# The causal masks of a state space scan: from a second TensorE product to a ScalarE copy in a PSUM bank of their own

## The chip, the cores and the metric

One core of a Trainium2 chip runs the whole program. The metric is the device time of one execution in microseconds (us). A matmul is issued on TensorE (PE, with its weight loads PEld); VectorE is DVE, ScalarE is ACT, GpSimd is POOL, SyncE is SP, and SP alone issues the transfers (DMA).

## The reference, cut to what matters

Two blocks follow each other. The first (attention with an index, latent attention, memory attention, experts in groups) ends before the change begins. The second has two layers: a bidirectional state space mixer (SSD) with an expert-choice layer (16 experts of 1024x1024, f32), then attention with a second expert-choice layer. The change lies in the SSD, of which this is the core:

```python
acum = jnp.cumsum(a, axis=-1)
tri = jnp.tril(jnp.ones((Q, Q), dtype=bool))
seg = jnp.exp(jnp.where(tri, acum[..., :, None] - acum[..., None, :], -jnp.inf))
cb = jnp.einsum('bclgn,bcsgn->bcgls', Cc, Bc)
y_diag = jnp.einsum('bcgrls,bcsgrp->bclgrp', cb[:, :, :, None] * seg, xdt)
```

It runs for context and latent tokens (256 each, chunks of 128), forwards and backwards, in 8 groups of 4 heads. `seg` on a diagonal chunk needs the causal mask, triangular one way for the forward scan and the other way for the backward scan.

## The kernel before, in words

The program is recorded in Python, and a scheduler then sets the order of each engine's instructions by its own simulated times: an instruction is placed when it would be ready, in favour of what was written earlier. So an edit at one place moves instructions of all engines from there on. Everything ahead of the SSD stands as before.

PSUM has eight banks of 128 x 512 f32. `self.ps(tag)` takes the next bank of a tag, `self.pb` says how many each tag has. From the SSD to the end of the first expert-choice layer the division is p=2, y=2, b=2, t=2 (`run`).

The SSD loops over the groups g = 0 to 7. `ssd_project` (L1462 on) makes six pieces of 128 channels: each splits its weights into a high and a low part (`split`, L1294 on ACT and L1295 on DVE, tiles `ws`, two buffers), multiplies them with the tokens in 24 matmuls (`mm3`, L1300 to L1302, tag p), and runs a five-tap convolution (ACT `pad`, `conv`, `xbc`; DVE L1506). `ssd_group` (L1522 on) transposes the pieces (tag t: L1530, L1535), makes `cb` (L1550, tag b) and then loops over the latent or context half q and the two chunks st. For each of these four steps it makes three exponents: two on the diagonal (d = 0 forwards, d = 1 backwards) and one off it. One exponent is a matmul into a bank of tag b (L1561, tiles `LBg` and `RR`); on the diagonal a second matmul adds the mask (L1564, `identb` times `maskb`, both bf16); ACT then takes the exponential into an SBUF tile `seg` (L1566, three buffers). POOL adds the two diagonal ones (L1568), DVE multiplies by `cb` into `M` (L1571), and TensorE applies M to the inputs (L1574, tag y). State products (L1586, L1592, L1597), sums and the spill of the group's result follow. While TensorE does group g's steps it also does the projections of group g+1, in the order that the scheduler set.

After the last group come the output projection (`ssd_out`, weights split again by L1294 and L1295, matmuls L1300 to L1302), the routing of the experts (tags t and b) and the expert products (L1817, tags p and y), whose weights arrive in `w` slots.

Of the kernel before, what the change touches and what calls it, by code (L numbers as in the profile page):

```python
# [22 lines left out]
AF = mybir.ActivationFunctionType  # L23
# [55 lines left out]
class Net:  # L79
# [11 lines left out]

    def ps(self, tag, n=512, dt=F32):
        self.n += 1
        return self.pp.tile([P, n], dt, tag=tag, name=f"ps{self.n}", bufs=self.pb[tag])

    @contextmanager
# [1214 lines left out]
    def ssd(self, right):  # L1311
        nc, a = self.nc, self.a
        self.piece = -1
        with self.pool("ssdh") as hp, self.pool("ssdx") as xp, self.pool("ssd") as pool, ExitStack() as q:
            tile_, x_ = self.cut(pool), self.cut(xp)
            pp = q.enter_context(self.pool("ssdq", "right"))
            self.ada_tile, self.ada_ps = lambda: self._t(pp, [P, 2 * D], "adaw", 1), "p"
            hT = [self.cut(hp)([P, 8, 512], f"hT{v}", 1, F32R) for v in range(2)]
            for r, xx in ((1, self.ctx_x), (0, self.x)):
                rows = self.norm_halves([xx[:, 0], xx[:, 1]], lambda: x_([P, 512], "xbc", 8), self.ctx_r if r else None)  # L1320
                m, sh = self.mod_cols(0, 0, r)
                self.to_features_mod(rows, m, sh, hT, (1 - r) * T, lambda: x_([P, 512], "z", 4)[:, :T])
            with self.pool("ssdr") as rp:
                self.load_const("const_b", rp)
                tmp_ = self.cut(rp)
                A4 = self.arena(rp, 3)
                self.ada_step(1)
                self.ssd_steps(tile_, tmp_, A4, hT)
            with self.pool("ssdg") as gp:
                self.yd = [self.dp.tile([P, 2, 512], F32, name=f"yd{g}") for g in range(7)]  # L1330
                self.sqa = self.cut(gp)([P, 512], "sqa")
                nc.gpsimd.memset(self.sqa, 0.0)
                for g in range(8):
                    parts = self.ssd_project(g, self.cut(pp), self.cut(xp), hT)
                    if g == 7:
                        q.close()
                        op = right.enter_context(self.pool("ssdo", "right"))
                        self.y7 = self.cut(op)([P, 2, 512], "y7")
                    self.ssd_group(g, *parts, self.cut(gp), self.cut(op) if g == 7 else None)
        return self.cut(op), op  # L1340
# [182 lines left out]
    def ssd_group(self, g, xs, BT, CT, zz, tile_, last=None):  # L1523
        nc = self.nc
# [21 lines left out]
        for q in range(2):  # L1546
# [7 lines left out]
            for st in range(2):  # L1554
# [2 lines left out]

                for d, var, lt, diag in ((0, 2 * q + st, st, True), (1, 2 * q + st, st, True),
                                         (st, 4 + q, 1 - st, False)):
                    p = self.ps("b").rearrange("p (r l) -> p r l", r=4)  # L1560
                    nc.tensor.matmul(p, lhsT=LBg[d][:, var * P:(var + 1) * P], rhs=self.RR[d][:, :, 2 * q + lt],  # L1561
                                     start=True, stop=not diag)
                    if diag:
                        nc.tensor.matmul(p, lhsT=self.identb, rhs=self.maskb[:, d], start=False, stop=True)  # L1564
                    e = tile_([P, 4, P], "seg", 3)
                    nc.scalar.activation(e, p, AF.Exp)  # L1566
                    ex.append((e, lt))
# [503 lines left out]
    def run(self):  # L2071
# [2 lines left out]
        self.small = "b"  # L2074
        nc = self.nc
        four = dict(p=2, y=2, b=2, t=2)
        with ExitStack() as right, self.psum(**four):
            out_, _ = self.ssd(right)
            ap = self.ctx.enter_context(self.pool("attt"))
            with self.pool("ch0") as pool, self.weight_slots(2), ExitStack() as more:  # L2080
# [71 lines left out]
```

## Time and profile before

| | us |
|---|---|
| median of 3 runs | 2182.82 |
| lowest, highest | 2179.14, 2183.91 |
| the profiled execution | 2178.93 |
| its span | 2177.1 |

The profile is of one execution. A page gives busy time by engine and 40 slices; a table by stage gives busy time, granted TensorE clock (PEclk, 1.00 is 2.4 GHz) and the share of DMA time for stretches that one chooses; a list of waits names the instruction that ended an engine's idle time. An instruction's duration on TensorE is not its cost in a full stream, since matmuls overlap: there the distance of the starts counts.

### The profile page before, as it was taken

How to read it: one execution, taken by the hardware profiler on the slowest of the kernel's cores; microseconds unless marked ns; L12 is line 12 of the kernel's file. 1: busy time of each engine (PE TensorE's matmuls, PEld its weight loads, DVE VectorE, ACT ScalarE, POOL GpSimd, SP SyncE). 2: the span in 40 equal slices, each digit the busy share in tenths (PEclk: the TensorE clock that was granted, in tenths of full speed). 3: DMA queues.
4: the chain of work that ended last, by engine and by line, in shares of the span. 5: the costliest groups of instructions: out<-in, count | busy, mean ns of one | idle time of the engine just before them, and what ended most of it. 6: DMA issues, size and time to landing. Idle time of an engine off the chain costs nothing. (4 is left out here: it accounts for less than half of the span.)

```text
span 2177.1 us, 23487 instructions
## 1 busy us (share of the span) xinstructions
PE 1882.8 (86%) x9000; PEld 1026.5 (47%) x9000; DVE 964.0 (44%) x1627; ACT 633.5 (29%) x1174; POOL 459.6 (21%) x481
## 2 busy tenths in 40 slices
PE   7989879988999999799899999997989767767666
PEld 6767644356767776567433333333756311111111
DVE  6776532278777777666222222222666301010101
ACT  6554421264444555444000000002454200000000
POOL 4340110033323333521011111111743100000000
PEclk9999989999999999999899999998999889898999
DMA  7554839843322222275799999997538699999996
GB/s 235 194 200 151 313 139 385 339 142 104 114 88 84 91 90 68 91 262 202 315 427 427 427 428 426 427 427 300 205 127 306 285 428 427 427 428 428 428 425 278
DMA packets 128565, 603.48 MB, mean 277 GB/s; under 512 B 18123, under 2 KB 58734, under 8 KB 87998
## 3 DMA queue, kind: packets, MB, share of 16 engines
q1 hardware_dynamic: 128446, 601.91, 69.8%
q8 instruction: 73, 1.20, 0.2%
q14 instruction: 46, 0.38, 0.1%
HBM read 597.09 MB, written 4.78 MB: 276 GB/s over the span
## 5 line engine op out<-in xcount | busy, mean ns | idle before, releaser
L1817 PE MATMUL ps<-w,xg 128*64 128x512 f32 (+1 forms) x2048 | 458.9, 648 | 106.1 <-DMA w<-in_moe_w_dram 106.1
L1817 PEld LDWEIGHTS ps<-w,xg 128*64 128x64 f32 (+1 forms) x2048 | 133.2, 129 | 392.8 <-issue 238.8
L1870 POOL TENSOR_TENSOR x<-x,o 128x512 f32<-128x512 f32 x24 | 38.9, 1623 | 651.2 <-DVE o L1869 651.2
L1300 PE MATMUL ps<-hT,ws 128*128 128x512 f32 x384 | 156.9, 409 | 6.3 <-DVE ada L1235 6.1
L1301 PE MATMUL ps<-hT,ws 128*128 128x512 f32 x384 | 156.9, 409 | 0.0
L1302 PE MATMUL ps<-hT,ws 128*128 128x512 f32 x384 | 155.3, 404 | 0.0
L1817 PE MATMUL ps<-w,ctx 128*32 128x512 f32 x512 | 109.1, 645 | 37.6 <-DMA w<-in_moe_w_dram 36.7
L1860 DVE SCALAR_TENSOR_TENSOR y<-ps,s,y 128x512 fp32r<-128x512 f32 x24 | 17.9, 748 | 247.5 <-ACT y L1859 247.5
L1817 PE MATMUL ps<-w,actT 128*64 128x512 f32 x512 | 123.5, 595 | 1.9 <-ACT actT L1855 1.9
L1506 DVE SCALAR_TENSOR_TENSOR conv<-pad,cols,conv 128x512 f32<-128x512 f32 x124 | 111.9, 903 | 2.6 <-ACT conv L1499 0.4
L1859 ACT ACTIVATE y<-ps,s 128x512 fp32r<-128x512 f32 x24 | 16.5, 686 | 322.8 <-PE ps L1817 246.4
L1300 PEld LDWEIGHTS ps<-hT,ws 128*128 128x128 f32 x384 | 72.7, 189 | 27.5 <-DVE ada L1235 6.8
L1869 DVE TENSOR_TENSOR o<-ps,g 128x512 f32<-128x512 f32 x80 | 52.3, 686 | 69.3 <-PE ps L1866 65.8
L1295 DVE TENSOR_TENSOR ws<-wr,ws 128x1024 fp32r<-128x1024 f32 x48 | 62.3, 1299 | 44.6 <-ACT ws L1294 38.0
L1301 PEld LDWEIGHTS ps<-hT,ws 128*128 128x128 f32 x384 | 72.8, 190 | 19.0 <-issue 3.8
L1302 PEld LDWEIGHTS ps<-hT,ws 128*128 128x128 f32 x384 | 72.7, 189 | 18.0 <-issue 1.9
L1817 PEld LDWEIGHTS ps<-w,ctx 128*32 128x32 f32 x512 | 25.9, 114 | 115.5 <-DMA w<-in_moe_w_dram 60.6
L1817 PEld LDWEIGHTS ps<-w,actT 128*64 128x64 f32 x512 | 43.4, 136 | 71.5 <-issue 67.0
L1568 POOL TENSOR_TENSOR seg<-seg,seg 128x512 f32<-128x512 f32 x32 | 47.4, 1481 | 116.1 <-ACT seg L1566 101.3
L1295 DVE TENSOR_TENSOR ws<-w,ws 128x1024 fp32r<-128x1024 f32 x46 | 61.5, 1343 | 19.9 <-ACT ws L1294 19.5
L1566 ACT ACTIVATE seg<-ps 128x512 f32<-128x512 f32 x96 | 54.8, 597 | 51.0 <-PE ps L1564 26.9
L1571 DVE TENSOR_TENSOR M<-seg,cb 128x512 f32<-128x512 f32 x64 | 53.7, 854 | 31.0 <-ACT seg L1566 20.7
(639 smaller groups left out, 3644.9 us busy)
## 6 DMA issues: line engine op xcount, KB each, us to landing
w<-in_moe_w_dram SPq DMA_DIRECT2D x164, 2048.0 KB
w<-in_moe_w_dram SPq DMA_DIRECT2D x56, 1024.0 KB
v<-in_ada_w_dram SPq DMA_DIRECT2D x16, 1024.0 KB
w<-in_moe_w_up_dram SPq DMA_DIRECT2D x16, 1024.0 KB
w<-in_moe_w_gate_dram SPq DMA_DIRECT2D x16, 1024.0 KB
w<-in_moe_w_down_dram SPq DMA_DIRECT2D x16, 1024.0 KB
wr<-in_ssd_in_w_dram SPq DMA_DIRECT2D x16, 1024.0 KB
w<-in_ssd_out_w_dram SPq DMA_DIRECT2D x32, 512.0 KB
```

The lines of the kernel that those rows point to most:

```text
L1295: (eng or self.nc.vector).tensor_tensor(lo, x, hi.bitcast(F32), op=OP.subtract)
L1300: t.matmul(p, lhsT=L[0], rhs=R[0], start=start, stop=False, **kw)
L1301: t.matmul(p, lhsT=L[0], rhs=R[1], start=False, stop=False, **kw)
L1302: t.matmul(p, lhsT=L[1], rhs=R[0], start=False, stop=stop, **kw)
L1506: nc.vector.scalar_tensor_tensor(seq(cv), pad[:, :, j:j + 256], tap(j), seq(cv), op0=OP.mult, op1=OP.add)
L1566: nc.scalar.activation(e, p, AF.Exp)
L1568: nc.gpsimd.tensor_tensor(ex[0][0], ex[0][0], ex[1][0], op=OP.add)
L1571: nc.vector.tensor_tensor(M[:, :, s], e, cb[:, st, None, s].to_broadcast([P, 4, P]), op=OP.mult)
L1817: nc.tensor.matmul(p[j * S:(j + 1) * S], lhsT=x(k, j), rhs=ws[j // ne][:, j % ne, k % nk, n * 512:(n + 1) * 512], start=(k == 0), stop=(k ...
L1860: nc.vector.scalar_tensor_tensor(y[:, 1], p, ws, y[:, 0].bitcast(F32), op0=OP.mult, op1=OP.subtract)
L1869: nc.vector.tensor_tensor(o, q, gr[s][:, c], op=OP.mult)
L1870: (nc.gpsimd if i else nc.vector).tensor_tensor(xx[:, i, c], xx[:, i, c], o, op=OP.add)
```

## The change

The masks of the diagonal exponents are no longer added by a matmul. One PSUM bank (tag m, tile `self.seg`) is set aside for all diagonal exponents. The very first time the mask goes in by the old identity matmul; the other 63 times ACT copies it from `maskb` into the bank (L1567 of the new file), and the exponents' matmul (L1568) adds onto it instead of starting afresh. Off-diagonal exponents stay on tag b. The division of the banks becomes p=2, y=2, b=3, m=1, from the SSD to the end of the first expert-choice layer; a tag that a division lacks, t here, falls to b.

```diff
     def ps(self, tag, n=512, dt=F32):
         self.n += 1
+        tag = tag if tag in self.pb else "b"
...
                 self.ssd_steps(tile_, tmp_, A4, hT)
+
+            self.seg = self.ps("m").rearrange("p (r l) -> p r l", r=4)
...
-                    p = self.ps("b").rearrange("p (r l) -> p r l", r=4)
+                    p = self.seg if diag else self.ps("b").rearrange("p (r l) -> p r l", r=4)
+                    if diag and (g, q, st, d) == (0, 0, 0, 0):
+                        nc.tensor.matmul(p, lhsT=self.identb, rhs=self.maskb[:, d], start=True, stop=True)
+                    elif diag:
+                        nc.scalar.activation(p, self.maskb[:, d], AF.Copy)
                     nc.tensor.matmul(p, lhsT=LBg[d][:, var * P:(var + 1) * P], rhs=self.RR[d][:, :, 2 * q + lt],
-                                     start=True, stop=not diag)
-                    if diag:
-                        nc.tensor.matmul(p, lhsT=self.identb, rhs=self.maskb[:, d], start=False, stop=True)
+                                     start=not diag, stop=True, skip_group_check=True)
...
-        with ExitStack() as right, self.psum(**four):
+        with ExitStack() as right, self.psum(p=2, y=2, b=3, m=1):
```

How the order moves: in the new file L1301 to L1303 are the projections (L1300 to L1302 before), L1533 the transposes (L1530), L1553 `cb` (L1550), L1568 the exponents (L1561), L1571 the exponentials (L1566), L1579 the products with M (L1574); the bank set aside is `ps1379_6544`.

On TensorE, the start of the fourth group, before (1790 is a projection, 1786 the modulation product that shares its banks):

```order
L1233 MATMUL ps1786_8460<-adaw_1785_8458,silu_c_336 32x512 x2
L1530 MATMUL ps1704_8109<-const_75,xbc_1672_7902 128x128 x4
L1561 MATMUL ps1717_8142<-RR0_1351_6452,LBg_1708_8126 128x512
L1564 LDWEIGHTS identb_1331_6366
L1564 MATMUL ps1717_8142<-maskb_1332_6368,identb_1331_6366 128x512
L1561 MATMUL ps1719_8147<-RR1_1369_6510,LBg_1710_8130 128x512
L1564 LDWEIGHTS identb_1331_6366
L1564 MATMUL ps1719_8147<-maskb_1332_6368,identb_1331_6366 128x512
L1530 MATMUL ps1705_8115<-const_75,xbc_1678_7944 128x128 x4
L1233 MATMUL ps1786_8460<-adaw_1785_8458,silu_c_336 32x512 x2
L1300 MATMUL ps1790_8472<-hT0_1281_6199,ws0_1788_8468 128x512
```

The two diagonal exponents of a step stand side by side in two banks, each with its mask, and a projection follows.

TensorE in the fourth group now, between the end of one projection (1763) and the start of the next (1816):

```order
L1303 MATMUL ps1763_8473<-hT0_1281_6199,ws1_1762_8470 128x512
L1553 MATMUL ps1691_8113<-xbc_1668_8008,xbc_1662_7966 128x256 x2
L1568 MATMUL ps1379_6544<-RR1_1369_6510,LBg_1687_8107 128x512
L1568 MATMUL ps1696_8127<-RR0_1351_6452,LBg_1685_8103 128x512
L1568 MATMUL ps1701_8147<-RR1_1369_6510,LBg_1687_8107 128x512
L1553 MATMUL ps1703_8158<-xbc_1668_8008,xbc_1662_7966 128x256 x2
L1568 MATMUL ps1708_8172<-RR0_1351_6452,LBg_1685_8103 128x512
L1568 MATMUL ps1379_6544<-RR0_1351_6452,LBg_1685_8103 128x512
L1579 MATMUL ps1689_8111<-M_1693_8118,xtm_1680_8085 64x256 x2
L1579 MATMUL ps1690_8112<-M_1693_8118,xtm_1680_8085 64x256 x2
L1568 MATMUL ps1379_6544<-RR1_1369_6510,LBg_1687_8107 128x512
L1301 MATMUL ps1816_8676<-hT0_1281_6199,ws0_1814_8672 128x512
```

Three diagonal exponents stand here with no projection between them, all in the one bank.

On ACT, the same place before:

```order
L1566 ACTIVATE seg_1718_8145<-ps1717_8142 128x512
L1566 ACTIVATE seg_1720_8150<-ps1719_8147 128x512
L1612 ACTIVATE xbc_1579_7478<-xbc_1579_7478,cols1_314 128x512
L1531 ACTIVATE xtm_1703_8108<-ps1705_8115 128x512
L1612 ACTIVATE xbc_1585_7520<-xbc_1585_7520,cols1_314 128x512
```

and now:

```order
L1295 ACTIVATE ws0_1820_8714<-wr_1818_8710 128x1024
L1556 ACTIVATE cb_1692_8116<-ps1691_8113 128x512
L1571 ACTIVATE seg_1695_8125<-ps1379_6544 128x512
L1571 ACTIVATE seg_1697_8129<-ps1696_8127 128x512
L1567 ACTIVATE ps1379_6544<-maskb_1332_6368 128x512
L1556 ACTIVATE cb_1704_8161<-ps1703_8158 128x512
L1511 ACTIVATE xbc_1747_8382<-conv_1746_8376 128x512
L1611 ACTIVATE z_1590_7634<-xbc_1564_7463 128x512
L1571 ACTIVATE seg_1699_8141<-ps1379_6544 128x512
L1611 ACTIVATE z_1594_7666<-xbc_1570_7505 128x512
L1617 ACTIVATE xbc_1564_7463<-xbc_1564_7463,cols1_314 128x512
L1567 ACTIVATE ps1379_6544<-maskb_1332_6368 128x512
```

Each copy stands behind the exponential that empties the bank, with other work of ACT between.

On TensorE, the start of the last group, before:

```order
L1561 MATMUL ps2091_9852<-RR0_1351_6452,LBg_2082_9836 128x512
L1564 LDWEIGHTS identb_1331_6366
L1564 MATMUL ps2091_9852<-maskb_1332_6368,identb_1331_6366 128x512
L1530 MATMUL ps2079_9825<-const_75,xbc_2050_9640 128x128 x4
L1561 MATMUL ps2093_9857<-RR1_1369_6510,LBg_2084_9840 128x512
```

and now:

```order
L1568 MATMUL ps1379_6544<-RR1_1369_6510,LBg_1942_9355 128x512
L1533 MATMUL ps2024_9770<-const_75,xbc_1995_9585 128x128 x4
L1538 MATMUL ps2026_9777<-const_75,xbc_2002_9630 128x128 x2
L1568 MATMUL ps1379_6544<-RR0_1351_6452,LBg_2027_9781 128x512
L1553 MATMUL ps2033_9791<-xbc_2008_9672,xbc_2002_9630 128x256 x2
L1579 MATMUL ps1944_9359<-M_1965_9431,xtm_1935_9333 64x256 x2
L1579 MATMUL ps1945_9360<-M_1965_9431,xtm_1935_9333 64x256 x2
L1568 MATMUL ps1379_6544<-RR1_1369_6510,LBg_2029_9785 128x512
```

The last group has no projection left beside it, before or now; its eight diagonal exponents now pass through the one bank.

## Rows read from the trace of the kernel before

**Rows 1.** The page, busy time by engine over the span.

```profile
PE 1882.8 (86%) x9000; PEld 1026.5 (47%) x9000; DVE 964.0 (44%) x1627; ACT 633.5 (29%) x1174; POOL 459.6 (21%) x481
```

**Rows 2.** By stage: length, busy of PE, PEld, DVE, ACT, POOL; clock, DMA, GB/s.

```profile
510.00:860.00 350.00, 346.44 (x1611) 252.29 (x1611) 269.14 (x330) 176.21 (x289) 107.86 (x140) 1.00 0.28 85
...
860.00:913.00 53.00, 43.43 (x198) 26.54 (x197) 34.13 (x41) 25.41 (x45) 27.69 (x28) 0.94 0.34 111
913.00:1024.00 111.00, 104.09 (x466) 81.82 (x465) 74.10 (x106) 52.17 (x71) 25.24 (x20) 1.00 0.59 202
1024.00:1042.00 18.00, 8.29 (x37) 5.07 (x37) 10.28 (x31) 5.56 (x8) 5.38 (x3) 0.70 0.98 398
...
1056.00:1400.00 344.00, 321.45 (x1326) 121.75 (x1323) 82.53 (x169) 26.90 (x49) 38.24 (x29) 0.98 1.01 426
```

**Rows 3.** TensorE by line, 510 to 860: count, busy and mean ns, idle before.

```profile
L1301 PE MATMUL ps<-hT,ws 128*128 128x512 f32 x330 | 135.3, 410 | 0.0
...
L1561 PE MATMUL ps<-RR,LBg 128*128 128x512 f32 x76 | 33.0, 460 | 0.0
...
L1564 PE MATMUL ps<-maskb,identb 128*128 128x512 bf16 x51 | 19.9, 390 | 0.0
```

**Rows 4.** TensorE in order of time near 859: start, duration, instruction.

```profile
858.41 0.39 PE L1300 MATMUL ps<-hT,ws 128*128 128x512 f32 x1
858.64 0.40 PE L1561 MATMUL ps<-RR,LBg 128*128 128x512 f32 x1
858.88 0.39 PE L1564 MATMUL ps<-maskb,identb 128*128 128x512 bf16 x1
858.92 0.58 PE L1301 MATMUL ps<-hT,ws 128*128 128x512 f32 x1
...
859.34 0.39 PE L1302 MATMUL ps<-hT,ws 128*128 128x512 f32 x1
```

**Rows 5.** Waits of TensorE, 510 to 860: total, times, longest.

```profile
PE ps L1300 <- DVE ada L1235: 3.2, 1, 3.2
```

**Rows 6.** ACT by line, 510 to 860: count, busy and mean ns, idle before.

```profile
L1294 ACT ACTIVATE ws<-wr 128x1024 fp32r<-128x1024 f32 x41 | 43.3, 1057 | 49.5 <-PE ps L1301 49.2
L1566 ACT ACTIVATE seg<-ps 128x512 f32<-128x512 f32 x75 | 42.8, 598 | 38.3 <-PE ps L1564 22.1 <-PE ps L1561 14.8 <-POOL seg L1568 1.0
L1499 ACT ACTIVATE conv<-ps,cols,cols 128x512 f32<-128x512 f32 x28 | 21.7, 774 | 2.2 <-DVE xbc L1509 2.2
L1508 ACT ACTIVATE xbc<-conv 128x512 f32<-128x512 f32 x27 | 17.1, 633 | 42.6 <-DVE conv L1506 29.1 <-issue 10.0 <-DMA yd<-xbc 3.4
L1496 ACT ACTIVATE pad<-ps 128x512 f32<-128x512 f32 x28 | 16.3, 582 | 0.4 <-ACT eF L1594 0.4
```

**Rows 7.** By stage, columns as in rows 2: behind the wait, and in the tail.

```profile
645.00:650.00 5.00, 5.00 (x15) 3.98 (x16) 4.76 (x7) 1.47 (x4) 0.02 (x1) 0.66 0.54 150
650.00:655.00 5.00, 5.00 (x26) 3.28 (x26) 2.21 (x3) 3.06 (x5) 1.39 (x3) 1.00 0.25 61
...
895.00:902.00 7.00, 5.98 (x20) 2.96 (x22) 2.36 (x3) 2.39 (x4) 1.61 (x2) 0.53 0.00 0
```

**Rows 8.** The last two groups in order of time, with idle time before.

```profile
866.36 1.02 PE L1550 MATMUL ps<-xbc,xbc 128*128 128x256 f32 x4
...
895.37 0.69 DVE L1571 TENSOR_TENSOR M<-seg,cb 128x512 f32<-128x512 f32 x1 [1.73 <-POOL seg L1568]
...
902.67 0.39 PE L1564 MATMUL ps<-maskb,identb 128*128 128x512 bf16 x1
...
903.10 1.08 ACT L1566 ACTIVATE seg<-ps 128x512 f32<-128x512 f32 x2 [1.22 <-PE ps L1564]
903.75 0.50 PE L1561 MATMUL ps<-RR,LBg 128*128 128x512 f32 x1 [0.46 <-ACT seg L1566]
903.84 1.28 POOL L1568 TENSOR_TENSOR seg<-seg,seg 128x512 f32<-128x512 f32 x1 [6.52 <-ACT seg L1566]
...
912.74 0.59 PE L1300 MATMUL ps<-ws,y 128*128 128x512 f32 x1
```

## The prediction

> **What bounds the kernel now.** First the page: TensorE is busy for 86% of the span, more than any other engine [rows 1], but that is an average. So the next view is the table by stage [rows 2]. In 510 to 860 us, the stretch in which groups one to seven are worked off, TensorE is busy for 346.4 of 350 us at the full clock, DVE for 269, ACT for 176, POOL for 108, and the transfers take 28%: TensorE sets the pace. In 860 to 913, the last two groups, nothing is full; there a chain from engine to engine sets the end. In 913 to 1024 the output projection keeps TensorE busy for 104 of 111 us. From 1024 to 1042 the latent tokens are routed, a chain on DVE and ACT, and from 1056 the weights of the experts stream at 1.01 of the transfer engines' time. That stream begins only when the slots are free and the routed tokens are there, and then runs at a fixed rate; so a microsecond won or lost before it comes out at its end. The waits of TensorE in 510 to 860 are one of 3.2 us [rows 5] and some tenths: there is no slack in which a removed product could vanish.
>
> **What the products of the mask cost.** Of the 64, 51 lie in 510 to 860 [rows 3]. Their duration of 390 ns is not their price, since matmuls overlap. From the start of the L1561 at 858.64 to that of the L1302 at 859.34 three matmuls pass, the mask's among them, in 0.70 us: 0.233 us each, as much as a projection's [rows 4], and no more for the change of type. 51 x 0.233 = 11.9 us, all of it on the path while TensorE is full. One product stays, before 510. The other 12 lie in the last two groups, where TensorE waits anyway: I count nothing for them, 12 x 0.233 = 2.8 us at the best.
>
> **What the copies cost.** ACT gains 63 copies of 128x512. The trace has no ACT write to PSUM; the nearest rows are a copy from PSUM (582 ns), the exponentials (598), a function from SBUF to SBUF (633) and one with two column operands (774) [rows 6]. I take 0.60, nearest to the plain ones, with 0.58 and 0.77 as the ends. In 510 to 860 that is 51 x 0.6 = 31 us, and ACT goes from 176 to 207 of some 340 us. It does not become the bound; the time is hidden under TensorE's projections, as long as ACT gets to a copy before TensorE gets to the product that waits for it.
>
> **The new wait.** One bank now holds every diagonal exponent in turn: copy, product, exponential, and only then the next copy. The shortest turn is 0.60 + 0.43 (from the start of a product to the exponential behind it, 902.67 to 903.10) + 0.58 and two handovers of under 0.1 us [rows 8]: about 1.75 us, 14 us for a group's eight turns, against some 48 us that a group has. What counts is therefore where the order puts the next product. TensorE executes in order, so behind a waiting L1568 all projections are queued, and ACT's weight splits and DVE wait for these. In the new order most diagonal products before the last two groups stand 20 to 35 rows apart, 4.6 to 7.7 us at 0.233 a matmul. ACT's work between, typically a split (1.06), a copy for the convolution (0.58), its scaled copy (0.77), an exponential and the mask's copy (0.6 each), takes 3.6 us [rows 6] from the end of a projection. So these waits should be met in time, with 1 to 3 us to spare.
>
> The exception is the fourth group, shown above: three diagonal products with hardly anything between. To the first of them ACT has a split, `cb`, two exponentials and the copy, 1.06 + 0.60 + 0.60 + 0.54 + 0.60 = 3.4 us, while TensorE has 1.9 us of work; to the second it has `cb`, three functions and a scaled copy of SBUF tiles, an exponential and a copy, about 4.4 us, against 1.5 us. TensorE waits 1.5 + 2.9 = 4.4 us there. Its counterpart before is the wait of 3.2 us at the same group's start, where the first projection had to wait for the modulation's sum on DVE [rows 5]. It cost more than itself: in the 5 us behind it the granted clock was 0.66 (partly the 1.2 GHz level), and TensorE began 15 matmuls where it began 26 in the next 5 us [rows 7], a loss of 11/26 x 5 = 2.1 us, 5.3 us in all. In the new order the modulation's product stands some 60 rows ahead of that place, so this wait should go. Old and new are about as dear: I count 0, with -5 (only the old one goes) and +6 (the old stays, the new comes, with a slow clock behind it) as the ends.
>
> **The tail.** In the last two groups there are no projections to fill the turns. In each step the backward exponential now follows the forward one not at once but after a copy and a product, 0.60 + 0.43 + 0.1 = 1.13 us later; POOL's sum (1.28), DVE's product (0.69 and more) and TensorE's follow as before [rows 8]. Seven steps stand behind the `cb` product of the second half of group seven (866.36 before), so the loss is 7 x 1.13 = 7.9 us where each is on the path and 0 where the chain waits for something else. Before, these 46.4 us (866.36 to 912.74) also hold waits for M, for transposes and a slow stretch (clock 0.53 in 895 to 902, near the 1.2 GHz level) [rows 7, 8], and about half of the steps are held by those. I take +4.
>
> **The rest.** Tags t and b together had four banks and now share three, without the diagonal exponents, which took 8 of b's 18 uses a group. That leaves 15 uses a group for three banks, five each, against nine for a bank of b and two and a half for one of t before; no wait is counted. In the routing the eight token products may rotate over three banks instead of two, while the transposes share them; the order there is nearly the same: 0, with 2 us either way. On SP's queue the spills of a group and the loads of the next change places by a few positions, with transfers at 28% [rows 2]; POOL's sums keep their sequence among themselves. Nothing in the attention or the second expert layer changes.
>
> **The sum.** -11.9 + 0 + 4 + 0 = -7.9 us. Against the profiled execution (2178.93, its span of 2177.1 and 1.8 around it) that is 2171; the profiled one is the fastest of those shown, 3.9 below the median, and the comparison goes by medians, so 2182.8 - 7.9 = 2175.
>
> **The rivals.** (1) *All of it arrives.* The tail hides its turns behind the waits it has anyway, the old wait goes and the new one is short: -11.9 - 3 = -15, 2168. For it speaks that TensorE is full at the full clock [rows 2]; against it the three products in a row.
> (2) *The tail and the fourth group eat it.* The tail costs its 7.9, the fourth group 4 or more on balance: -11.9 + 8 + 4 = 0, 2183 (2179 to 2187 count as no change, since a measurement of this kernel can tell about 0.2% from none).
> (3) *The one bank becomes the pace.* Each of the 51 turns in the full stretch makes TensorE wait, because ACT comes late to exponential and copy behind splits and convolution work that themselves wait for TensorE (49 us of such waits before the splits [rows 6]). The gain is gone from 0.23 us a turn on; at 0.5 us it is 51 x 0.5 - 11.9 + 4 = +18, 2200. Against it stand the 20 to 35 rows between the products. The Trainium skill, page Perfetto Trace Analysis, section Matmuls, says that independent products should rotate through different banks, so that emptying one overlaps the next product; this change does the opposite for the diagonal, and by that rule this rival would be the outcome.
> That the change does not do what it says can be left out: the order shows 63 copies and one mask product.
>
> **How the numbers follow.** The sum as forecast, -4.4 to -12: 0.48. Rival 1, beyond -12: 0.13. Rival 2, within 4.4 either way: 0.23. Rival 3, slower by more: 0.16. So faster 0.61, same 0.23, slower 0.16. The range goes from 2166, the whole gain with the old wait gone, to 2188, where rival 2 ends and rival 3 begins; below it lies some 0.05, above it some 0.14.
>
> **What the changed profile would show.** Right: the stretch of the full TensorE shorter by 10 to 13 us at a busy share as high as before; copies near 0.6 us; TensorE's named waits for ACT's copies only in the fourth group and the tail; the tail 2 to 8 us longer than 46.4; the expert stream begun some 8 us earlier. Wrong: many small waits for `ps` from ACT, 0.2 us or more a turn, spread over all groups (rival 3); a tail over 8 us longer or a long slow clock behind the fourth group (rival 2); or an earlier end of the SSD that the routing gives back, which my zero for the banks of t and b would have missed.

## The result: slower by half a per cent

The changed kernel takes 2192.32 us (2188.86 to 2194.07), the kernel before 2180.69 us on the same chip: a ratio of 1.0054, with 1.0042 to 1.0066 as its 95% interval, or 11.6 us more. I had forecast 2175, and 2166 to 2188 as the range. The profiled execution's span went from 2177.1 to 2189.0, 11.9 us.

The page of the changed kernel, busy time by engine, answers to [rows 1]:

```profile
PE 1874.5 (86%) x8937; PEld 1036.1 (47%) x8937; DVE 968.8 (44%) x1627; ACT 666.6 (30%) x1237; POOL 448.2 (20%) x481
```

TensorE has 63 matmuls less, ACT 63 instructions more. The change does what it says, and TensorE is busy for less time; the time is lost between its instructions. The stages, with the columns of [rows 2]:

```profile
510.00:860.00 350.00, 336.18 (x1543) 249.18 (x1542) 263.19 (x327) 194.40 (x326) 94.75 (x132) 0.98 0.27 83
860.00:913.00 53.00, 42.70 (x169) 26.62 (x167) 34.32 (x37) 34.76 (x63) 30.91 (x35) 0.84 0.38 126
913.00:1024.00 111.00, 101.56 (x450) 78.15 (x451) 70.82 (x104) 51.30 (x68) 21.01 (x18) 0.98 0.58 202
1024.00:1042.00 18.00, 12.76 (x64) 9.56 (x62) 10.68 (x23) 9.41 (x16) 7.73 (x8) 0.99 0.56 223
1056.00:1400.00 344.00, 314.56 (x1316) 126.96 (x1314) 83.27 (x158) 26.37 (x49) 34.37 (x27) 0.99 0.98 415
```

In the stretch that was full, 346.4 of 350 us at the full clock, TensorE is now busy for 336.2 us at 0.98. In the two last groups its clock is 0.84, where it was 0.94. The waits of TensorE that are named, in 510 to 860 us (total, times, longest), answer to [rows 5]:

```profile
PE ps L1579 <- DVE M L1576: 10.7, 3, 6.3
PE ps L1301 <- DVE ada L1236: 1.2, 1, 1.2
```

and in 860 to 930 us:

```profile
PE ps L1579 <- DVE M L1576: 7.2, 5, 3.2
PE ps L1568 <- ACT ps L1567: 1.7, 1, 1.7
```

So TensorE does not stand before the exponents' product, waiting for a copy. It stands further down the chain, behind the exponential, POOL's sum and DVE's product, before the product with M. The longest wait is that of the fourth group, to which the prediction had given a place of its own. The changed kernel in order of time there, all engines (start, duration, what ended the idle time before):

```profile
704.17 2.63 POOL L1588 TENSOR_TENSOR xw<-xtm,coef 128x256 f32<-128x256 f32 x2
704.18 1.08 ACT L1571 ACTIVATE seg<-ps 128x512 f32<-128x512 f32 x2
...
705.13 0.62 ACT L1567 ACTIVATE ps<-maskb 128x512 f32<-128x512 bf16 x1
...
705.31 1.50 PE L1568 MATMUL ps<-RR,LBg 128*128 128x512 f32 x3
...
705.65 0.61 ACT L1556 ACTIVATE cb<-ps 128x512 f32<-128x512 f32 x1
706.13 0.65 ACT L1511 ACTIVATE xbc<-conv 128x512 f32<-128x512 f32 x1
706.25 1.10 DVE L1576 TENSOR_TENSOR M<-seg,cb 128x512 f32<-128x512 f32 x1
...
706.65 0.65 ACT L1611 ACTIVATE z<-xbc 128x512 f32<-128x512 f32 x1
706.76 1.17 POOL L1607 TENSOR_TENSOR xbc<-xbc,eF 128x256 f32<-128x256 f32 x1
707.44 0.60 ACT L1571 ACTIVATE seg<-ps 128x512 f32<-128x512 f32 x1
707.89 1.26 POOL L1573 TENSOR_TENSOR seg<-seg,seg 128x512 f32<-128x512 f32 x1
707.96 1.74 DVE L1608 TENSOR_TENSOR xbc<-xbc,z 128x512 f32<-128x512 f32 x1 [0.61 <-POOL xbc L1607]
709.11 3.38 POOL L1615 TENSOR_TENSOR sqa<-sqa,z 128x512 f32<-128x512 f32 x2
709.62 1.75 DVE L1512 SCALAR_TENSOR_TENSOR xbc<-xbc,conv 128x512 f32<-128x512 f32 x1
...
711.29 1.75 DVE L1576 TENSOR_TENSOR M<-seg,cb 128x512 f32<-128x512 f32 x1
...
713.10 1.12 PE L1579 MATMUL ps<-M,xtm 128*64 128x256 f32 x4 [6.28 <-DVE M L1576]
```

ACT is in time. By the order of ACT shown ahead of the prediction, the two exponentials at 704.18 are this step's backward one and the one off the diagonal; the copy at 705.13 and the exponential at 707.44 already belong to the next step. What holds M are the queues of POOL and DVE. POOL's sum starts at 707.89, 3.1 us after the backward exponential has ended (0.6 us behind its start), behind two products for the states (L1588) and a sum for the group before (L1607). It ends at 709.15, and the diagonal part of M then stands on DVE behind a product for the group before (L1608) and the last step of a convolution (L1512), which take 1.74 and 1.75 us. From the backward exponential to the product with M it is 8.9 us (704.18 to 713.10). TensorE has issued all that stands ahead of the product with M, the three products at 705.31 last (the order of TensorE shown ahead of the prediction has only two of these), and waits for 6.3 us. Behind the wait the clock is lower for a while; the stages around it, columns as above:

```profile
700.00:705.00 5.00, 5.00 (x25) 3.29 (x24) 2.64 (x3) 3.82 (x7) 2.90 (x4) 1.00 0.00 0
705.00:713.00 8.00, 1.80 (x6) 0.62 (x4) 7.38 (x7) 5.75 (x11) 7.42 (x6) 0.84 0.52 164
713.00:717.00 4.00, 3.90 (x13) 2.38 (x14) 0.69 (x3) 1.17 (x3) 0.49 (x1) 0.50 0.17 66
717.00:722.00 5.00, 5.00 (x23) 3.80 (x23) 3.15 (x4) 1.76 (x5) 1.53 (x3) 0.97 0.00 0
```

In the 4 us behind the wait the granted clock is 0.50, the 1.2 GHz level. The end of the SSD shows in the products with M, of the changed kernel and, on the second line, in that of before (first and last start):

```profile
L1579 PE MATMUL ps<-M,xtm x256: 378/379/690, 532.7 to 921.6; 128*64 128x256 f32 x128
```

```profile
L1574 PE MATMUL ps<-M,xtm x256: 379/379/689, 534.2 to 910.6; 128*64 128x256 f32 x128
```

They begin 1.5 us earlier and end 11.0 us later.

**Where the time comes from.** To follow it, TensorE's matmuls are numbered in order of time, the masks' products left out, and each one's start is compared with that of the same number in the kernel before. In us, later is positive, at these times of the kernel before (the experiments, e1 and on, follow below):

| | 660 | 720 | 860 | 920 | 1060 | 1900 |
|---|---|---|---|---|---|---|
| changed kernel | -4.7 | +3.0 | +1.5 | +9.9 | +7.0 | +11.8 |
| e1 division alone | -10.2 | -9.3 | -5.3 | -15.2 | -9.6 | -8.4 |
| e3 one bank, masks by matmul | -7.0 | -7.6 | -8.9 | -15.4 | -17.0 | -16.5 |
| e4 no masks, old division | -4.1 | -7.2 | -7.1 | -4.6 | -4.3 | -4.3 |
| e5 no masks, b=4 | -15.4 | -15.2 | -16.9 | -26.3 | -25.1 | -18.5 |
| e6 two banks, copies | -10.4 | -13.1 | -15.5 | -27.3 | -26.6 | -27.0 |
| e9 forward only | -11.7 | -13.9 | -15.8 | -25.8 | -28.7 | -25.5 |
| e10 not the first step | -12.2 | -14.4 | -16.0 | -12.6 | -18.6 | -15.8 |
| e12 other sequence | -7.8 | -0.6 | +1.2 | +5.4 | +0.9 | +4.5 |
| e13 not the last step | -11.5 | -13.7 | -20.4 | -25.5 | -28.1 | -24.4 |

The changed kernel is ahead until the fourth group's wait (7.7 us between 660 and 720), does no better than even up to 860, and loses 8.4 us in the last two groups.

### The profile page after: what moved, and what is told of

Its sections match the earlier page's. It is cut to its first block, busy times and chain, and to the rows that moved or that the text cites. A ratio compares the mean times of both kernels' runs of the same rounds, so it can differ in the third digit from the quotient of the medians.

```text
span 2189.0 us, 23429 instructions
## 1 busy us (share of the span) xinstructions
PE 1874.5 (86%) x8937; PEld 1036.1 (47%) x8937; DVE 968.8 (44%) x1627; ACT 666.6 (30%) x1237; POOL 448.2 (20%) x481
## 5 line engine op out<-in xcount | busy, mean ns | idle before, releaser
L1301 PE MATMUL ps<-hT,ws 128*128 128x512 f32 x384 | 157.0, 409 | 2.9 <-DVE ada L1236 1.2
L1302 PE MATMUL ps<-hT,ws 128*128 128x512 f32 x384 | 155.7, 406 | 0.0
L1303 PE MATMUL ps<-hT,ws 128*128 128x512 f32 x384 | 154.1, 401 | 0.0
L1864 ACT ACTIVATE y<-ps,s 128x512 fp32r<-128x512 f32 x24 | 16.5, 687 | 317.9 <-PE ps L1822 247.1
L1509 DVE SCALAR_TENSOR_TENSOR conv<-pad,cols,conv 128x512 f32<-128x512 f32 x124 | 101.9, 822 | 2.8 <-ACT conv L1502 0.8
L1301 PEld LDWEIGHTS ps<-hT,ws 128*128 128x128 f32 x384 | 73.2, 191 | 25.0 <-issue 3.1
L1822 PEld LDWEIGHTS ps<-w,actT 128*64 128x64 f32 x512 | 48.8, 136 | 76.1 <-issue 59.1
L1302 PEld LDWEIGHTS ps<-hT,ws 128*128 128x128 f32 x384 | 73.1, 190 | 17.3 <-issue 1.5
L1303 PEld LDWEIGHTS ps<-hT,ws 128*128 128x128 f32 x384 | 73.0, 190 | 17.6 <-issue 1.2
L1576 DVE TENSOR_TENSOR M<-seg,cb 128x512 f32<-128x512 f32 x64 | 65.8, 1048 | 26.5 <-ACT seg L1571 24.7
L1295 ACT ACTIVATE ws<-wr 128x1024 fp32r<-128x1024 f32 x48 | 50.7, 1057 | 62.6 <-PE ps L1302 55.6
```

The costliest lines, as they stand in the source:

```text
L1295: self.nc.scalar.activation(hi, x, AF.Copy)
L1301: t.matmul(p, lhsT=L[0], rhs=R[0], start=start, stop=False, **kw)
L1302: t.matmul(p, lhsT=L[0], rhs=R[1], start=False, stop=False, **kw)
L1303: t.matmul(p, lhsT=L[1], rhs=R[0], start=False, stop=stop, **kw)
L1509: nc.vector.scalar_tensor_tensor(seq(cv), pad[:, :, j:j + 256], tap(j), seq(cv), op0=OP.mult, op1=OP.add)
L1576: nc.vector.tensor_tensor(M[:, :, s], e, cb[:, st, None, s].to_broadcast([P, 4, P]), op=OP.mult)
```

## The experiments

Two theories were told apart. **One**, the shared bank: the serial turn of the one bank costs time in itself. **Two**, the pace: slow turns make the steps fall behind the projections; these run ahead, and later there is nothing left to fill TensorE's waits. Against both, rivals: the new division, ACT's load, the accident of an order. Each kernel's time stands beside the kernel before, at 2180 to 2181 in every set.

**e1: the division alone.**

```diff
+        tag = tag if tag in self.pb else "b"
...
-        with ExitStack() as right, self.psum(**four):
+        with ExitStack() as right, self.psum(p=2, y=2, b=4):
```

> The kernel before with only the banks divided anew: p=2, y=2, b=4, where the transposes' tag t falls to b; masks by the identity matmul as before, every exponent in a rotating bank of b. Theory (the one bank of the diagonal exponents costs the time, because the backward exponent of a step must wait until the forward one is read out and the mask copied, so M comes late and TensorE stands before the product with M): 2181, within 4 us of the kernel before. Rival one (the shared division of t and b costs the time): about 2190.

2169.55, ratio 0.9951 (0.9937 to 0.9964): faster by 11 us, which neither side had. The division does not cost the time, and something in it, or in the order that came with it, gains.

**e2: two mask banks.**

```diff
-            self.seg = self.ps("m").rearrange("p (r l) -> p r l", r=4)
+            self.seg = [self.ps("m").rearrange("p (r l) -> p r l", r=4) for _ in range(2)]
...
-                    p = self.seg if diag else self.ps("b").rearrange("p (r l) -> p r l", r=4)
-                    if diag and (g, q, st, d) == (0, 0, 0, 0):
+                    p = self.seg[d] if diag else self.ps("b").rearrange("p (r l) -> p r l", r=4)
+                    if diag and (g, q, st) == (0, 0, 0):
...
-        with ExitStack() as right, self.psum(p=2, y=2, b=3, m=1):
+        with ExitStack() as right, self.psum(p=2, y=2, b=2, m=2):
```

> The changed kernel with two mask banks, one for the forward and one for the backward exponents (m=2), and b=2 for everything else, t included; 62 copies by ScalarE. Theory (one shared bank): copy and product of the backward exponent run beside the forward ones, the waits of 3 and 6 us before the product with M go, and the time is 2169 to 2176. Rival one (the division with t in b): still fewer banks in b, 2190 or more. Rival two (the load of the copies on ScalarE): the copies are all there, so 2188 to 2193.

2163.34, ratio 0.9922 (0.9909 to 0.9936), 6 us under what the theory asked. All the copies are there, so ACT's load (rival two) falls for this order. It has a loss of its own in the preparation of the scan: its clock in 495 to 512 us is 0.60, where the kernel before has 1.00.

```profile
495.00:512.00 17.00, 14.25 (x46) 8.75 (x47) 16.75 (x33) 3.04 (x7) 13.55 (x13) 0.60 0.54 177
```

**e3: one bank, masks by matmul.**

```diff
...
-                    elif diag:
-                        nc.scalar.activation(p, self.maskb[:, d], AF.Copy)
...
-                                     start=not diag, stop=True, skip_group_check=True)
+                                     start=True, stop=not diag)
+                    if diag:
+                        nc.tensor.matmul(p, lhsT=self.identb, rhs=self.maskb[:, d], start=False, stop=True)
```

> The changed kernel with its one bank for all diagonal exponents, but the masks added by the identity matmul as before; no copy on ScalarE. Theory (one shared bank): the serial turn stays, shorter by the copy, and the 11.9 us of mask products come back, so clearly slower than the kernel before, 2186 to 2200. Rival two (the copies on ScalarE): 2181, as before.

2161.97, ratio 0.9911 (0.9897 to 0.9924): 18 us faster than before, with every mask product and one bank. This was the clearest miss, and theory one falls in that form: one bank alone is harmless here. No product with M waits over 1 us up to the last group.

**e4: no masks, on the old division.**

```diff
-                                     start=True, stop=not diag)
-                    if diag:
-                        nc.tensor.matmul(p, lhsT=self.identb, rhs=self.maskb[:, d], start=False, stop=True)
+                                     start=True, stop=True)
...
-                    nc.scalar.activation(e, p, AF.Exp)
+                    nc.scalar.activation(e, p, AF.Exp, scale=0.01)
```

> The kernel before without the mask matmuls, which leaves the causal masks out of the computation (the exponential gets a scale of 0.01 so that it stays finite); banks as before. It measures what the 64 products are worth. By my step of 0.233 us a product: 11.9 us in the full stretch and 0 to 2.8 in the last two groups, so 2166 to 2170. Rival three (whatever shortens the stretch is given back by a new order of the engines' queues): 2176 to 2185.

2175.92, ratio 0.9982 (0.9973 to 0.9991): rival three's 4.5 us. With neither a copy nor a bank of its own the same wait is there, in 510 to 860 us:

```profile
PE ps L1572 <- DVE M L1569: 6.0, 2, 3.6
```

So it is not the bank as such that brings it: also in an order that merely lacks the mask products, M's product can stand too near.

**e5: no masks, b=4.** The edits of e1 and e4 together.

> The division p=2, y=2, b=4 with masks left out of the computation (the exponential again scaled by 0.01). In the order of this kernel the projections stand no more than 70 matmuls into the next group when a group's last product with M is done (kernel before 171 to 240, changed kernel 216 to 284). Theory two (the pace of the steps against that of the projections: where a step's chain is slow, the projections run ahead, and the last groups are left with nothing to fill TensorE's waits): here nothing runs ahead, so the 64 products show their full worth against the same division with masks (2169.6), 12 to 15 us: 2154 to 2158. Rival three (a removed product is given back by the order anyway, as in the run without masks on the old division, 4.5 us): 2163 to 2168.

2160.8, ratio 0.9912 (0.9899 to 0.9926), 8.8 us under e1: between what theory two and the rival had asked. By the table e5 is 11.6 us ahead of e1 at 860, 11.1 at 920 and 15.5 at 1060, of which 5 are given back in the expert layer. Up to the end of the SSD the products are thus worth what I had counted for this pair of kernels, 11.9, and nothing more in the last two groups; what comes on top comes in the output projection and the routing.

**e6: two mask banks, and t in m outside the groups.** As e2, with `self.fall` set to "m", and to "b" inside the group loop.

```diff
-        tag = tag if tag in self.pb else "b"
+        tag = tag if tag in self.pb else self.fall
```

> The kernel with two mask banks and the copies; tag t falls to the two banks of m outside the group loop (in the preparation of the scan, in the output projection and the routing) and to b only inside it. The run with two banks had lost 11 us near 500 us, in the preparation, where b had two banks for everything. Theory two: that loss goes and the rest stays, 2150 to 2156. Rival (the loss comes from a new order of the preparation for another reason): 2161 to 2166.

2154.17, ratio 0.988 (0.9864 to 0.9896), as expected. TensorE is full at the full clock, with 57 copies of 609 ns in the stretch:

```profile
510.00:860.00 350.00, 350.00 (x1635) 258.77 (x1634) 274.93 (x349) 213.15 (x363) 108.70 (x147) 1.00 0.27 86
...
L1570 ACT ACTIVATE ps<-maskb 128x512 f32<-128x512 bf16 x57 | 32.8, 609 | 0.4
```

The Trainium skill, page Perfetto Trace Analysis, section Matmuls, has independent products rotate through different banks. Between the changed kernel and e6 the traces agree with it (38 us); e3, fast on one bank, shows that the rule does not decide alone.

**e7: every copy twice.**

```diff
                         nc.scalar.activation(p, self.maskb[:, d], AF.Copy)
+                        nc.scalar.activation(p, self.maskb[:, d], AF.Copy)
```

> The changed kernel with every mask copied twice by ScalarE, so that each turn of the one bank is 0.6 us longer and ScalarE has 38 us more to do. Theory two (a turn's length sets the pace of the steps): the projections run still further ahead, and in the bare last two groups 16 turns are longer by 0.6 us: 2200 to 2206. Rival (only the order of the queues happened to be bad, the turn does not matter): within 4 us of the changed kernel, 2188 to 2196.

2228.69, ratio 1.0218 (1.0205 to 1.0232): 36 us over the changed kernel, 0.58 us for each of the 63 doubled turns. Theory two's sign, more than twice its size. On average that is the length of the second copy. Now TensorE also waits before the exponents' product, in 510 to 930 us:

```profile
PE ps L1580 <- DVE M L1577: 10.9, 4, 4.7
PE ps L1569 <- ACT seg L1572: 6.0, 4, 2.9
PE ps L1569 <- ACT cb L1556: 5.6, 5, 1.7
```

**e8: six buffers for the pieces.**

```diff
...
-            o = xt_([P, 512], "xbc", 8)
+            o = xt_([P, 512], "xbc", 6)
```

The other place that takes buffers of this name (L1321) is changed in the same way.

> The changed kernel with six instead of eight buffers for the convolved pieces (xbc), nothing else: the copies, the one bank and the division stay. The projections cannot run as far ahead: at a group's last product with M they stand 180 to 221 matmuls into what follows, instead of 216 to 284, and between the first product with M of group six and the last of group seven there are 167 matmuls instead of 111. Theory two: the 50 projections that stand there now fill waits, about 12 us: 2178 to 2184. Theory one (the serial turn of the one bank costs the time where it stands, whatever runs beside it): 2190 or more, since fewer buffers can only add waits.

2196.28, ratio 1.0071 (1.0059 to 1.0084): theory two's number failed, and the time lies where theory one had put it. Fewer buffers brought new waits in 510 to 860 us:

```profile
PE ps L1234 <- ACT conv L1502: 5.1, 4, 1.8
PE ps L1579 <- DVE M L1576: 4.6, 2, 3.4
PE ps L1591 <- ACT seg L1571: 3.3, 1, 3.3
```

In the last two groups alone it did as hoped: from 860 to 920 it loses 0.6 us on the kernel before (13.7 to 14.3 by the numbered matmuls), where the changed kernel loses 8.4.

**e9: only the forward exponents in the bank.**

```diff
-                    p = self.seg if diag else self.ps("b").rearrange("p (r l) -> p r l", r=4)
+                    own = diag and d == 0
+                    p = self.seg if own else self.ps("b").rearrange("p (r l) -> p r l", r=4)
...
-                                     start=not diag, stop=True, skip_group_check=True)
+                                     start=not own, stop=own or not diag, skip_group_check=own)
+                    if diag and not own:
+                        nc.tensor.matmul(p, lhsT=self.identb, rhs=self.maskb[:, d], start=False, stop=True)
```

> The changed kernel, but only the forward exponents use the bank set aside and the copies (31 copies, 1 + 32 mask products); the backward ones take a bank of b and the mask product. A step then has one turn of the bank, not two in a row. Theory two (two turns with a copy between them make M late and let the projections run ahead): nothing runs ahead (at most 96 matmuls at a group's last product with M), and 31 x 0.233 = 7 us of products go, against the division alone (2169.6): 2160 to 2166. Rival two (each copy on ScalarE costs its share): halfway between the division alone and the changed kernel, 2178 to 2184.

2153.37, ratio 0.987 (0.9852 to 0.9888), better than expected, and with e6 the fastest of all. One turn of the bank a step does no harm in this order; two in a row in every step, each with a copy, go with the slow orders (the changed kernel, e7, e8), though e10 and e13 keep them in three of four steps. TensorE is full:

```profile
510.00:860.00 350.00, 350.00 (x1673) 260.30 (x1673) 287.38 (x352) 199.75 (x339) 118.36 (x152) 1.00 0.28 86
```

**e10: not in the first step.** As e9 with `own = diag and (d == 0 or q + st > 0)`.

> The changed kernel with one thing undone: in the first of a group's four steps the backward exponent takes a bank of b and the mask product; 55 of 63 copies stay. The waits of 3.3 and 6.3 us before the product with M stood in first steps, each with 3.4 us lost to the half clock behind it (6.8 us at half). In the new order M's product stands at least 31 matmuls behind its last exponent in groups zero to six, where it stood 7. Theory two, by place: these 16 us go, 1.9 us of products come back, 2172 to 2180. Rival (every turn costs its share): 8 of 63 copies, 2188 to 2192.

2164.18, ratio 0.9928 (0.9913 to 0.9942): 28 us gained on the changed kernel by taking 8 of 63 copies out. An even price per turn (the rival) is out of the question. The waits before the products with M of 3.3 and 6.3 us are gone; nine are left, the longest 1.1:

```profile
PE ps L1582 <- DVE M L1579: 3.0, 9, 1.1
```

**e11: the copies beside the turn.**

```diff
+                    if diag:
+                        nc.scalar.activation(e, self.maskb[:, d], AF.Copy)
                     nc.scalar.activation(e, p, AF.Exp)
```

(on e3)

> The one bank with the masks by matmul (2162.0), plus 64 copies of the masks by ScalarE, of the same size, into the SBUF tile of the exponential, where nobody reads them: ScalarE has the load of the changed kernel, but the copy is not between one exponential and the next product. If the copy costs because it stands in the turn: 2160 to 2168. If it costs as ScalarE's time: near 2185 or more.

2172.5, ratio 0.9962 (0.9947 to 0.9976): 10.5 over e3, between the two. ACT's time was not free in this order, or the order itself cost it (e14 and e15 show that 5 to 7 us can come from that alone). Not decided.

**e12: another sequence of the same instructions.**

```diff
-                for d, var, lt, diag in ((0, 2 * q + st, st, True), (1, 2 * q + st, st, True),
-                                         (st, 4 + q, 1 - st, False)):
+                for d, var, lt, diag in ((0, 2 * q + st, st, True), (st, 4 + q, 1 - st, False),
+                                         (1, 2 * q + st, st, True)):
...
```

The sums that follow take their operands by the new places.

> The changed kernel with the same instructions, recorded in another sequence: forward exponent, the one off the diagonal, backward exponent. It tests how much of the result is the accident of one order. In this order the projections run as far ahead (221 to 286 matmuls), and the first steps of groups three and five have M's product 7 and 8 matmuls behind the last exponent. Theory two: the same turns, 2187 to 2197. Rival (accident of the order): more than 6 us away from 2192 on either side.

2181.28, ratio 1.0003 (0.9993 to 1.0013): 11 us under the changed kernel, so by the mark set ahead the order is a good part of it. The waits are of the same kind, in 510 to 860 us:

```profile
PE ps L1579 <- DVE M L1576: 7.5, 3, 5.1
PE ps L1568 <- ACT ps L1567: 3.6, 3, 2.2
```

**e13: not in the last step.** As e10 with `own = diag and (d == 0 or q + st < 2)`.

> The changed kernel with the backward exponent of the last of a group's four steps (second half, second chunk) on a bank of b with the mask product; 55 of 63 copies stay, as when the first step was taken out (2164.2). If the time was lost because the first steps' two turns come one behind the other (by place): those stay as they are, 2184 to 2192. If it was lost because the order put M's product 7 to 14 matmuls behind its last exponent wherever the chain of turns had fallen behind: in the new order no product with M in groups zero to five stands nearer than 32, no wait of over 1 us before M there, and 2166 to 2174; the last two groups run without projections (105 matmuls after the last projection, as before) and give nothing.

2156.61, ratio 0.9895 (0.988 to 0.991), 9 us under the expected range. Not the place of the turns decides; relief in the first step and relief in the last both did it. In the stretch no product with M waits as much as 0.4 us. It also goes against theory two: the projections run up to 240 matmuls ahead at the end of groups, as in the kernel before, and its last two groups are the better for it (43.6 us from the first product with M of group seven to the last, 52.5 in the changed kernel).

**e14 and e15: how much a sequence is worth.** The edit of e12 on the kernel before, and on e9.

> The kernel before with its own instructions recorded in the sequence forward, off the diagonal, backward. How much does an order alone move a kernel in which no exponent waits for a copy? In its order M's product stands 17 matmuls or more behind the last exponent up to group five. If the sensitivity belongs to the turns of the one bank: within 4 us of 2180. If every order is a draw of this size (11 us in the changed kernel): more than 6 us away.

> The forward-only kernel (2153.4) recorded in the sequence forward, off the diagonal, backward; M's product at least 20 matmuls behind the last exponent in groups zero to six. If slack in the order is what counts: within 4 us of 2153. If every order is a draw: more than 6 us away.

e14: 2173.39, ratio 0.9972 (0.9958 to 0.9986), 7.5 us under its parent; e15: 2158.57, ratio 0.989 (0.9871 to 0.9908), 5.2 over its own, between the two marks. So an order alone moves this program by 5 to 11 us, whatever is in it; that is as much as the whole of the expected gain.

**The kernels side by side.** For each, from its profiled execution: how near the product with M stands to its exponents, as the smallest number of matmuls, mask products included, from the third exponent of a step to the first product with M, in the first six groups (the exponents are counted off in threes in order of time; by a step's own last exponent, mask products left out, some numbers differ, 2 in e7, 9 in e4 and 25 to 31 in e3, e9, e10 and e13, and the classes stay); the pauses of TensorE from 505 us to the last product with M (of each pair of matmuls whose starts lie over 0.8 us apart, what is over 0.4); the time at half clock in 505 to 930 us.

| | copies | median us | nearest M | pauses us | half clock us |
|---|---|---|---|---|---|
| before | 0 | 2180.7 | 27 | 13.2 | 10.2 |
| changed kernel | 63 | 2192.3 | 9 | 29.6 | 34.1 |
| e1 | 0 | 2169.6 | 27 | 7.7 | 3.4 |
| e3 | 0 | 2162.0 | 31 | 3.9 | 3.4 |
| e4 | 0 | 2175.9 | 7 | 15.8 | 34.1 |
| e6 | 62 | 2154.2 | 28 | 2.3 | 6.8 |
| e7 | 126 | 2228.7 | 8 | 53.5 | 51.2 |
| e8 | 63 | 2196.3 | 10 | 35.0 | 41.0 |
| e9 | 31 | 2153.4 | 33 | 3.7 | 3.4 |
| e10 | 55 | 2164.2 | 33 | 16.6 | 10.2 |
| e12 | 63 | 2181.3 | 9 | 25.1 | 23.9 |
| e13 | 55 | 2156.6 | 43 | 8.9 | 0.0 |
| e14 | 0 | 2173.4 | 21 | 12.9 | 17.1 |

What separates them is the third column: where the nearest product with M stands 10 matmuls or fewer behind its exponents, there are long waits before M and 24 to 51 us at half clock; at 27 or more it is about 10 us or less; e14 lies between, with 21 and 17.1. Ten matmuls are 2.3 us at 0.233, and from the backward exponential to the product with M it took 8.9 us in the rows above. All four kernels with both diagonal exponents of every step in one bank behind copies are in the first class; so is e4, with none. e2 (28), e5 (27), e11 (32) and e15 (31), with under 8 us at half clock, fit in as well. The last two groups, where the projections run out, are left out: in the seventh the kernel before itself has a product with M 10 matmuls behind its exponents, and it does not wait. So the long waits of the first six groups stand at near products, but a near product does not bring a wait by itself.

## Why the prediction was wrong

**The products: right by one pair of kernels.** 51 x 0.233 = 11.9 us; e5 against e1 measures 11.6 at 860 us. Two other pairs give less there, e4 against the kernel before 7.1 and e6 against e3 6.6; since the order differs in each pair as well, the close agreement of the first is partly luck.

**The copies: right in price.** 0.60 us; the 49 in 510 to 860 us took 610 ns:

```profile
L1567 ACT ACTIVATE ps<-maskb 128x512 f32<-128x512 bf16 x49 | 29.9, 610 | 0.6
```

That their time is hidden held in e6; e11 leaves it open for other orders.

**The old wait: right.** It went, and took about what I had worked out (5.3 us): from 640 to 660 us e1 and e3, which keep all mask products, gain 6.3 and 6.2 us on the kernel before. But I had it offset by the new one, and it was not an offset of equals.

**The new wait: the step that failed.** I compared the distance from one diagonal product to the next with ACT's work between, found 1 to 3 us to spare, and was right about that: no named wait for a copy before 860. But I followed the chain only to the exponents' product. It goes on over the exponential, POOL's sum and DVE's M to the product with M, behind whatever stands in the queues of POOL and DVE, and that product I did not look up in the order, though it is in the rows of the fourth group that I had shown (L1579): in the changed kernel it stood as near as 9 matmuls behind the exponents, in the kernel before never nearer than 27 in the first six groups. To the fourth group I gave 4.4 us without the clock; it was 6.3 us and 4 us at 0.50 behind it, after a like wait of 3.3 us in the third group. With the products and the old wait gone and nothing new, the kernel would have been some 11.6 + 6.2 = 17.8 us ahead at 860 us; it was 1.5 behind. By this estimate the new waits and the clock behind them cost about 19 us in this stretch, where I had put 4.4; the waits before M are 10.7 us of it.

**The tail: mis-sized.** +4, with 7.9 as the upper end. From the `cb` product of the second half of group seven to the first projection behind the last M it took 56.5 us (865.93 to 922.44) against 46.4 [rows 8], so +10.1; by the numbered matmuls it is 8.4 from 860 to 920 us, of which 2.9 are made up by 1060. The waits before M are 7.2 us where they had been 0.9, but the kernel before had waited for banks in their place. Its waits in 860 to 930 us:

```profile
PE ps L1561 <- ACT seg L1566: 5.8, 6, 1.4
...
PE ps L1574 <- DVE M L1571: 0.9, 1, 0.9
```

All named waits of TensorE there add up to 14.5 us now and 11.6 before. More of the loss is the clock, which was not in my price of a turn. The same stretch before and, on the second line, now:

```profile
860.00:930.00 70.00, 58.45 (x262) 38.13 (x261) 45.27 (x51) 34.34 (x58) 35.45 (x34) 0.95 0.33 110
860.00:930.00 70.00, 55.22 (x222) 35.48 (x221) 44.10 (x49) 43.11 (x77) 39.10 (x42) 0.85 0.28 95
```

A mean of 0.95 is 7 us of the 70 at half clock, 0.85 is 21; the 14 us more cost up to 7 us (an estimate: half of them).

**The division: right that it costs nothing, wrong that it is worth nothing.** e1 gained 11 us, all of which may be the order's accident (5 to 11 us, by e12, e14 and e15).

**Behind the SSD** the changed kernel loses another 5 us between 1060 and 1900 (+7.0 to +11.8), and e5 gives back 6.6. I counted on a gain or loss coming out unchanged at the end of the expert stream; which transfers or waits take it was not followed.

**The rivals.** Rival 3 had the outcome's sign and nearly its size (2200). Its mechanism, a small wait for ACT at each of 51 turns, is not what happened; the waits are few, long, before M, and made dearer by the clock. Its chance of 0.16 was too low, because I took a free place behind the copy for a free chain. Rival 2 had the places, the fourth group and a tail over 8 us longer, and its sign, a slow clock behind the fourth group, was there; its price (2183) was too low by 9 us, and the third group's wait was not in it.

**What stays open.** Why the scheduler puts M's product so near is argued, not shown: the long waits of the changed kernel stand where the projections of the next group had just been used up, so that there was nothing else ready to place. e13, where they ran as far ahead without harm, and e8, where they could not and it did not help, say that this is not the whole of it. No run took work off POOL or DVE, whose queues held M in the rows above, so how much of the waits is theirs was not measured. And of the 11.6 us some 5 to 11 may belong to this one order: e12, with the same instructions, came out level with the kernel before.

## What to carry to other kernels

When a change lengthens a chain, follow it to the last engine that executes in order and count there, in the new order, what stands between the chain's start and its consumer: here, while the projections ran, 27 matmuls were enough and 10 were not. Price a pause of TensorE with the half clock behind it. Where a scheduler sets the order, one build is a draw, worth 5 to 11 us here; a gain of that size needs the same instructions in a second sequence, and the cheap remedy, two banks or one turn a step (1.2% under the kernel before), was found by relieving the chain, not by counting the work saved: e3, which saves no work, is 0.9% under it.

## What the runs showed of the hardware

ACT writes a mask into PSUM about as fast as it copies the same size out of it (582 ns, [rows 6]): 579 to 637 ns for 128x512 from bf16, 609 on average.

M's instruction on DVE (128x512, two operands in SBUF) takes 0.68 us where POOL runs nothing meanwhile (33 of 64 in the changed kernel), and 1.49 on average where POOL is busy for over half of it (29 of 64). In the rows above DVE's three at 1.74 and 1.75 us stand beside POOL's sums, one of 1.26 us and two that take 3.38 together. If each of the three took the 0.68 of an M alone, the wait of 6.3 would be some 3 us shorter (an estimate: 3 x 1.07). The Trainium skill, page SBUF — State Buffer, section Summary: rules for kernel authors, says that a DVE instruction with two SBUF inputs and a GpSimd instruction that reads SBUF do not run at once, the second to issue blocks until the first ends; the durations agree with that, no run here takes the two apart.
